# A delta rule in chunks: output as a stream of its own, and the inverse applied after the state's part

## The chip, the cores and the metric

The kernel runs on one core of a Trainium2 chip. The metric is the time of one execution on the device in microseconds (us). Engines are named as in the profile: PE is the tensor engine's matmul, PEld its weight load, DVE the vector engine, ACT the scalar engine, POOL is GpSimd, SP the queue that only issues DMAs. Each engine works through its own queue in order and waits there for what others have to deliver.

## What is computed

One inference step of a hybrid layer: 16 meta rows and 2048 prompt frames, and beside them 64 frames of a running stream. The input is projected; one half of the heads is latent attention, the other a gated delta rule with 4 heads of 128 x 128 state; then an output projection and an MLP. The delta rule is evaluated in chunks (here of 128 rows; 16 for the meta rows, 64 for the running stream, 18 chunks in all). Cut to what matters:

```python
decay = exp(where(causal, gc[:, None] - gc[None, :], -inf))     # gc: cumulative sum of g
a = where(strict, (k * beta) @ k.T * decay, 0)
t_inv = inverse(eye + a)
u = t_inv @ (v * beta)
w = t_inv @ (k * beta * exp(gc))
qk = q @ k.T * decay
# from chunk to chunk, with the state S:
v_new = u - w @ S
o = (q * exp(gc)) @ S + qk @ v_new
S = S * exp(gc[-1]) + (k * exp(gc[-1] - gc)).T @ v_new
# o is then normalised per row and multiplied by a gate
```

## The kernel before

The program has stages that follow each other: input projection and convolution (`phase_a`), the delta rule (`phase_g`), attention, attention of the running stream, output projection and MLP. The change is in `phase_g`, which runs from 519 to 950 us of the profile.

`phase_g` is written as generators that a loop advances in rounds; a `yield` ends a stream's part of a round. Three kinds of stream run side by side. `gdn_prep` prepares a chunk without needing the state: it loads k, v and q (L446, L448), transposes k and v (L455, L474), makes the decay matrix `dm` (L461, L463) and its scaled form `db`, normalises k (`rk`, `kn`, L485), forms the matrix to be inverted (`bn`, L500) and `qk` (L502), inverts by doubling over seven levels (`lev`, first mask L521, then L529 to L557), and ends with `uf`, the inverse (L574), and `wt`, the inverse's transpose applied to `kneg` = -k exp(gc) (L523, L578, L580). Up to four chunks are in preparation at once. `gdn_scan` takes one prepared chunk at a time, in six parts: `pv` = `uf` by `vn` (L598) plus `wt` by the state (L599) in one accumulation, `vw` (L601); the new state (L605, L607); the output's share of the state (L619, L621); its share of the chunk (L627, L629) with the row norm; the scaling on POOL (L638); the transpose (L642), the gate (L644) and the store. The third stream, `q_gen` (L728 to L742), projects and rotates the queries of attention in 17 tiles of five parts, and after it `keys` makes attention's first keys; one part of it is taken in each round after round `QS` = 5.

A new chunk is taken up at the earliest `GR` = 6 rounds after the one before, with at most `GK` = 4 in preparation and `GA` = 5 ahead of the scan. PSUM has five banks for the preparation (`gpp` in the trace), two for the scan (`gps`) and one for the queries. The order in which instructions stand in each engine's queue is then made by a scheduler, which follows the order of the code where it sees nothing better; operands are read by their names in the rows (`lev`, `bn`, `kn`, `vn`, `uf`, `vw`, `S`). Names and numbers of the constants are at L45 to L57.

Of the kernel before, what the change touches and what calls it, by code (L numbers as in the profile page):

```python
# [8 lines left out]
F32 = mybir.dt.float32  # L9
F32R = mybir.dt.float32r  # L10
# [36 lines left out]
GB = {"kq": 4, "qk": 5, "kd": 5, "vn": 5, "uf": 5, "wt": 5, "ss": 5, "kv": 2, "sq": 1, "kn": 1, "lg": 1, "dm": 2, "db": 1, "bn": 1,  # L47
      "kneg": 3, "bh": 4, "bl": 4, "tt": 5, "uu": 5, "q16": 2, "rk": 3, "se": 1, "vw": 2, "S": 3, "o1": 1, "o": 1, "fr": 2}
GR, GK, GA, GF, GL0 = 6, 4, 5, 2, 4
QSB, QS = 2, 5  # L50
# [60 lines left out]
def bc1(ap, p, a, b):  # L111
    return ap.unsqueeze(1).to_broadcast([p, a, b])
# [6 lines left out]
class Prog:  # L119
# [255 lines left out]
    def gdn_consts(self, es):  # L375
        nc, I = self.nc, self.I
        c = self.pool(es, "g_const")
        t = lambda name, shape, dt=F32: c.tile(list(shape), dt, name=name)
        self.m_le, self.m_gt = t("m_le", (128, 128)), t("m_gt", (128, 128))
# [6 lines left out]
        self.sct = {k: t(k, (128, nch, 4)) for k in ("beta", "nbeta", "g", "egc", "negc", "egl")}  # L386
        self.sc = {n: {k: v[:, i, :] for k, v in self.sct.items()} for i, n in enumerate(CHUNKS)}

    def gdn_setup(self):
# [32 lines left out]
        flat = lambda t: t.rearrange("p a b -> p (a b)")  # L422
        ps = self.aps.tile([128, NB], F32, name="ps", tag="ps", bufs=APB)
# [14 lines left out]
    def gdn_prep(self, n, P):  # L438
# [10 lines left out]
        lg = self.gt("lg", 2)  # L449
        nc.gpsimd.tensor_tensor(lg[:C, :, :C], bc1(self.m_gt[:C, :C], C, 4, C), bc2(sc["g"][:C], C, 4, C), op=ALU.mult)  # L450
# [9 lines left out]
        for h in range(4):  # L460
            nc.tensor.matmul(pe[:C, h, :C], lg[:C, h, :C], self.m_le[:C, :C], start=True, stop=True)  # L461
# [15 lines left out]
        if want_o:  # L477
            sq = self.gt("sq", 2)
            nc.scalar.activation(sq[:, :, :C], kq[:, :, 1, :C], AF.Square)
# [42 lines left out]
        kneg = self.gt("kneg", 1)  # L522
        nc.gpsimd.tensor_tensor(kneg[:C], kn[:C], bc2(sc["negc"][:C], C, 4, 128), op=ALU.mult)  # L523
# [57 lines left out]
        P.update(kq=kq, ss=ss, qk=qk, kd=kd, vn=vn, uf=uf, wt=wt)  # L581

    def gdn_scan(self, n, P):
# [17 lines left out]
        nc.vector.tensor_tensor(vw[:C], pv[:C], bc2(sc["beta"][:C], C, 4, 128), op=ALU.mult)  # L601
        yield
# [11 lines left out]
        if n == 0:  # L614
            return
        yield
        po = self.gpsum("s")
        for h in range(4):
            nc.tensor.matmul(po[:C, h, :], P["kq"][:, h, 1, :C], st[:, h, :], start=True, stop=True)  # L619
# [6 lines left out]
        for h in range(4):  # L626
            nc.tensor.matmul(po[:C, h, :], P["qk"][:C, h, :C], vw[:C, h, :], start=True, stop=True)  # L627
# [3 lines left out]
        for h in range(4):  # L631
            nc.scalar.activation(o1[:C, h, :], o[:C, h, :], AF.Square, accum_out=ss[:C, 4 + h:5 + h])
        fr = self.gt("fr", 1, (128, 12))
# [14 lines left out]
    def phase_g(self, g=True, q=True, eb=None):  # L648

        with ExitStack() as es:  # L650
# [12 lines left out]
            preps, scan, started, scanned, rounds = [], None, 0, 0, 0  # L663
            began = [-GL0] * NL
            while g and scanned < len(CHUNKS):
# [6 lines left out]
                if rounds > QS:  # L672
# [8 lines left out]
                if scan is None and "uf" in Ps[scanned]:  # L681
# [1249 lines left out]
```

## Time and profile before

| | before |
|---|---|
| median of 3 runs | 3322.38 us (3321.15 to 3323.21) |
| the profiled execution | 3322.66 us |
| its span | 3320.9 us |
| PE busy in the span | 96% |
| DVE, ACT, POOL busy | 80%, 47%, 12% |
| delta-rule stage, 519 to 950 us | 431 us |
| PE, DVE, POOL, ACT busy in the stage | 376.8, 310.5, 235.7, 214.5 us |

A row of the profile's timeline says when an instruction (or several of one kind) started, how long it took, the engine, the line of the kernel, what it writes and reads, and in brackets how long the engine sat idle before it and what ended that. A PE instruction's duration includes its way through the array, so what one costs the queue is the distance to the next start. PE needs two passes for one f32 product of this stage, so four heads appear as x8.

### The profile page before, as it was taken

How to read it: one execution, taken by the hardware profiler on the slowest of the kernel's cores; microseconds unless marked ns; L12 is line 12 of the kernel's file. 1: busy time of each engine (PE TensorE's matmuls, PEld its weight loads, DVE VectorE, ACT ScalarE, POOL GpSimd, SP SyncE). 2: the span in 40 equal slices, each digit the busy share in tenths (PEclk: the TensorE clock that was granted, in tenths of full speed). 3: DMA queues.
4: the chain of work that ended last, by engine and by line, in shares of the span. 5: the costliest groups of instructions: out<-in, count | busy, mean ns of one | idle time of the engine just before them, and what ended most of it. 6: DMA issues, size and time to landing. Idle time of an engine off the chain costs nothing.

```text
span 3320.9 us, 54512 instructions
## 1 busy us (share of the span) xinstructions
PE 3196.8 (96%) x20037; PEld 2943.1 (89%) x20037; DVE 2650.8 (80%) x5438; ACT 1558.4 (47%) x3495; POOL 400.5 (12%) x758
## 2 busy tenths in 40 slices
PE   9999998998979999999899999999999999999999
PEld 6888887888867778887799999999999999999999
DVE  8877654788758788888789888888888888988887
ACT  5555524555536868787564222334333333422232
POOL 0100013675510000000201000011000002100000
PEclk9999998999978999999999999999999999999999
DMA  4322213233221011010332222233222225122222
GB/s 132 91 74 70 74 63 100 87 104 100 59 57 35 20 34 34 25 37 26 106 99 75 77 77 75 76 110 109 88 76 73 65 73 160 58 73 77 77 74 70
DMA packets 318091, 248.09 MB, mean 75 GB/s; under 512 B 31776, under 2 KB 291616, under 8 KB 317760
## 3 DMA queue, kind: packets, MB, share of 16 engines
q1 hardware_dynamic: 300256, 219.21, 22.8%
q10 hardware_dynamic: 15536, 16.23, 1.6%
q0 software_dynamic: 2032, 9.18, 0.8%
q8 instruction: 157, 2.57, 0.3%
q14 instruction: 110, 0.90, 0.1%
HBM read 196.99 MB, written 47.52 MB: 74 GB/s over the span
## 4 chain that ended last, share of the span: by engine, by line
PE 83%; DVE 8%; ACT 2%; DMA 2%; issue 2%; POOL 1%; SPq 0%; POOLq 0%; DVEq 0%; ACTq 0%
PE psu L1601 23%; PE psd L1601 21%; PE ps L270 5%; PE ps L271 5%; PE ps L272 5%; PE pss L994 2%; PE pso L1011 2%; PE pss L995 2%; PE pss L996 2%; PE pso L1013 2%; PE pso L1012 2%; PE pspre L964 2%; DVE hl L1581 0%; PE psm L889 0%; DMA qh<-mrow 0%
## 5 line engine op out<-in xcount | busy, mean ns | idle before, releaser
L1601 PE MATMUL psu<-hh,uh 128*128 128x352 f32 x1728 | 563.0, 326 | 2.6 <-ACT uh L1497 2.1
L1601 PE MATMUL psu<-hl,uh 128*128 128x352 f32 x1728 | 557.3, 323 | 0.0
L1601 PE MATMUL psu<-hh,ul 128*128 128x352 f32 x1728 | 549.9, 323 | 0.0
L1601 PE MATMUL psd<-al,dh 128*128 128x352 f32 x1536 | 496.0, 323 | 3.5 <-DVE al L1790 3.2
L1601 PE MATMUL psd<-ah,dl 128*128 128x352 f32 x1536 | 494.6, 322 | 0.0
L1601 PE MATMUL psd<-ah,dh 128*128 128x352 f32 x1536 | 473.3, 324 | 11.1 <-DVE y L1709 7.4
L1709 DVE TENSOR_TENSOR y<-y,psd 128x352 f32<-128x352 f32 x768 | 386.6, 515 | 103.5 <-PE psd L1601 101.5
L1601 PEld LDWEIGHTS psu<-hh,uh 128*128 128x128 f32 x1728 | 325.7, 189 | 4.5 <-ACT uh L1497 2.5
L1601 PEld LDWEIGHTS psu<-hl,uh 128*128 128x128 f32 x1728 | 326.1, 189 | 1.2 <-issue 0.5
L1601 PEld LDWEIGHTS psu<-hh,ul 128*128 128x128 f32 x1728 | 323.9, 188 | 0.2 <-DVE ul L1475 0.2
L270 PE MATMUL ps<-hhi,whi 128*128 128x512 f32 (+5 forms) x880 | 313.6, 360 | 9.7 <-ACT hhi L134 7.1
L272 PE MATMUL ps<-hhi,wlo 128*128 128x512 f32 (+5 forms) x880 | 314.0, 358 | 0.0
L271 PE MATMUL ps<-hlo,whi 128*128 128x512 f32 (+5 forms) x880 | 312.5, 356 | 0.3 <-DVE hlo L135 0.2
L1601 PEld LDWEIGHTS psd<-ah,dh 128*128 128x128 f32 x1536 | 284.1, 188 | 16.9 <-DVE y L1709 11.5
L1601 PEld LDWEIGHTS psd<-al,dh 128*128 128x128 f32 x1536 | 289.1, 188 | 5.5 <-DVE al L1790 5.4
L1497 ACT CAST dh<-wr 128x512 fp32r<-128x512 f32 x192 | 119.3, 621 | 367.2 <-PE psd L1601 324.8
L1601 PEld LDWEIGHTS psd<-ah,dl 128*128 128x128 f32 x1536 | 288.8, 188 | 0.0
L1788 ACT CAST ah<-u 128x352 fp32r<-128x352 f32 x192 | 93.4, 487 | 398.6 <-DVE u L1786 280.0
L135 DVE TENSOR_TENSOR Pl<-P,Ph 128x512 fp32r<-128x512 f32 (+4 forms) x352 | 211.2, 611 | 52.2 <-ACT Ph L134 49.7
L998 ACT ACTIVATE P<-pss 128x512 f32<-128x512 f32 (+4 forms) x352 | 185.9, 539 | 87.6 <-PE pss L996 76.9
L965 DVE TENSOR_REDUCE mp<-pspre 128x1 f32<-128x296 f32 (+6 forms) x400 | 189.1, 500 | 31.1 <-PE pspre L964 29.2
L1714 POOL TENSOR_TENSOR y<-y,v 128x352 f32<-128x352 f32 x40 | 40.8, 1043 | 1330.8 <-DVE y L1709 1330.7
(458 smaller groups left out, 7266.5 us busy)
## 6 DMA issues: line engine op xcount, KB each, us to landing
wr<-in_w_up SPq DMA_DIRECT2D x192, 256.0 KB
wr<-in_w_down SPq DMA_DIRECT2D x192, 256.0 KB
qn<-scr_qN SPq DMA_DIRECT2D x32, 384.0 KB
wr<-in_w_out SPq DMA_DIRECT2D x48, 256.0 KB
wraw<-in_w_in SPq DMA_DIRECT2D x42, 256.0 KB
scr_convT<-s SPq DMA_DIRECT2D x36, 256.0 KB
mixr<-scr_mixT SPq DMA_DIRECT2D x12, 704.0 KB
out_y_T<-y SPq DMA_DIRECT2D x48, 176.0 KB
```

Of the source, the lines that this page charges most:

```text
L135: (lo_eng or nc.vector).tensor_tensor(lo, src, hi.bitcast(F32), op=ALU.subtract)
L270: nc.tensor.matmul(ps[:m, :n], whi[:, k, :m], hi[:, k], start=k == 0, stop=False)
L271: nc.tensor.matmul(ps[:m, :n], whi[:, k, :m], lo[:, k], start=False, stop=False)
L272: nc.tensor.matmul(ps[:m, :n], wlo[:, k, :m], hi[:, k], start=False, stop=k == 7)
L964: nc.tensor.matmul(ps[:, :z - a], qh[:r, i * 128:(i + 1) * 128], kh[:r, a:z], start=True, stop=True)
L965: nc.vector.tensor_reduce(m[:, i:i + 1] if one else mp[:, j:j + 1], ps[:, :z - a], axis=AX.X, op=ALU.max)
L994: nc.tensor.matmul(ps[:w, off:], kh[:r, s:s + w], qh[:r, off:], start=True, stop=False)
L998: nc.scalar.activation(p[:w, off:], ps[:w, off:], AF.Exp)
L1497: self.nc.scalar.copy(t[0], src)
L1601: self.nc.tensor.matmul(ps, w, h, start=i == 0, stop=i == len(steps) - 1)
L1709: adds.append(nc.vector.tensor_tensor(Y[j][:, d], Y[j][:, d], ps, op=ALU.add).ins)
L1788: done = nc.scalar.copy(A[f, j][0], u).ins
```

## The change

- `wt` and `kneg` are gone. The scan first multiplies the normalised keys by the state (`pk`), scales by -exp(gc) on DVE (`vk`), adds the values on POOL (`vr`), and applies the inverse once, to the sum (`pv`).
- The output is a generator of its own, `gdn_out`, in five parts; the scan has four, one of them empty. An output of a chunk is advanced in each round beside the scan of the next.
- The decay matrix: g is split into a rounded part `gh` and a rest `gl`; the mask `m_le` times each is made on POOL (two `lg` instead of one), and two fp32r matmuls of 512 columns take the place of four f32 ones of 128.
- In `gdn_prep` the norm's `rk`, its use in `kn`, and the square of q stand in other rounds than before.
- The third stream starts after round 2 instead of 5 and skips every sixth round. Six buffers of `kq` instead of four, two of `sq` and `lg` instead of one.

```diff
-GR, GK, GA, GF, GL0 = 6, 4, 5, 2, 4
-QSB, QS = 2, 5
+GR, GK, GA, GF, GL0, QE = 6, 4, 5, 2, 4, 6
+QSB, QS = 2, 2
...
+        nc.scalar.copy(self.sct["gh"], gg)
+        nc.vector.tensor_tensor(self.sct["gl"], gg, self.sct["gh"].bitcast(F32), op=ALU.subtract)
...
-        lg = self.gt("lg", 2)
-        nc.gpsimd.tensor_tensor(lg[:C, :, :C], bc1(self.m_gt[:C, :C], C, 4, C), bc2(sc["g"][:C], C, 4, C), op=ALU.mult)
+        lg = [self.gt("lg", 2, dt=F32R) for _ in range(2)]
+        for x, g in zip(lg, (sc["gh"].bitcast(F32), sc["gl"])):
+            nc.gpsimd.tensor_tensor(x[:C, :, :C], bc1(self.m_le[:C, :C], C, 4, C), bc2(g[:C], C, 4, C), op=ALU.mult)
...
-        for h in range(4):
-            nc.tensor.matmul(pe[:C, h, :C], lg[:C, h, :C], self.m_le[:C, :C], start=True, stop=True)
+        for i, x in enumerate(lg):
+            nc.tensor.matmul(pe[:C, :, :C], self.m_gt[:C, :C], x[:C, :, :C], start=i == 0, stop=i == 1)
...
+        if want_o:
+            sq = self.gt("sq", 2)
+            nc.scalar.activation(sq[:, :, :C], kq[:, :, 1, :C], AF.Square)
+        yield
         rk = self.gt("rk", 2, (128, 12))
...
-        yield
         tv = self.gpsum()
...
+        yield
         kn = self.gt("kn", 2)
...
-        kneg = self.gt("kneg", 1)
-        nc.gpsimd.tensor_tensor(kneg[:C], kn[:C], bc2(sc["negc"][:C], C, 4, 128), op=ALU.mult)
...
-        yield
-        ps = self.gpsum()
-        for h in range(4):
-            nc.tensor.matmul(ps[:, h, :C], kneg[:C, h, :], uf[:C, h, :C], start=True, stop=True)
-        wt = self.gt("wt", 2)
-        nc.scalar.copy(wt[:, :, :C], ps[:, :, :C])
...
+        pk = self.gpsum("s")
+        for h in range(4):
+            nc.tensor.matmul(pk[:C, h, :], P["kq"][:, h, 0, :C], st[:, h, :], start=True, stop=True)
+        vk = self.gt("vk", 1)
+        nc.vector.tensor_tensor(vk[:C], pk[:C], bc2(sc["negc"][:C], C, 4, 128), op=ALU.mult)
+        vr = self.gt("vr", 1)
+        nc.gpsimd.tensor_tensor(vr[:C], vk[:C], P["vn"][:C], op=ALU.add)
+        yield
+        yield
         pv = self.gpsum("s")
         for h in range(4):
-            nc.tensor.matmul(pv[:C, h, :], P["uf"][:C, h, :C], P["vn"][:C, h, :], start=True, stop=False)
-            nc.tensor.matmul(pv[:C, h, :], P["wt"][:, h, :C], st[:, h, :], start=False, stop=True)
+            nc.tensor.matmul(pv[:C, h, :], P["uf"][:C, h, :C], vr[:C, h, :], start=True, stop=True)
...
-        if n == 0:
-            return
-        yield
+
+    def gdn_out(self, n, P):
...
-                if rounds > QS:
+                if rounds > QS and rounds % QE:
...
+                if outs and next(outs[0], "x") == "x":
+                    outs.pop(0)
                 if scan is not None and next(scan, "x") == "x":
+                    if CHUNKS[scanned]:
+                        outs.append(self.gdn_out(CHUNKS[scanned], Ps[scanned]))
                     scan, scanned = None, scanned + 1
```

Where instructions stand now. On DVE, around the inverse's first mask of a late chunk (`lev<-m_lv,bn`; `gpp` and `gps` are PSUM banks), before:

```order
L634 TENSOR_SCALAR fr<-ss 128x4
L500 TENSOR_TENSOR bn<-gpp,db 128x256
L502 TENSOR_TENSOR qk<-gpp,dm 128x256
L644 SCALAR_TENSOR_TENSOR o_10181<-gps,g_out,ga 128x512
L521 COPY_PREDICATED lev_4990<-m_lv,bn 128x512
L601 TENSOR_TENSOR vw<-gps,beta 128x512
```

and on DVE there now:

```order
L507 TENSOR_TENSOR bn<-gpp,db 128x256
L509 TENSOR_TENSOR qk<-gpp,dm 128x256
L528 COPY_PREDICATED lev_4994<-m_lv,bn 128x512
L641 TENSOR_TENSOR o<-o_10143,gps 128x512
L600 TENSOR_TENSOR vk<-gps,negc 128x512
L562 CAST uu<-gpp 128x4x64
```

The output's gate product (L644) no longer stands ahead of the mask (L521, now L528), and `vk` is new behind it; the scan's `vw` has moved elsewhere.

On POOL, in the same part of the program, from the normalised keys' product `kd` on, before:

```order
L523 TENSOR_TENSOR kneg<-kn,negc 128x512
L525 TENSOR_TENSOR kd<-kn,dm 128x512
L638 TENSOR_TENSOR o<-o,fr 128x512
L507 TENSOR_TENSOR bl<-bn,bh 128x512
L595 TENSOR_TENSOR se<-S,egl 128x512
L450 TENSOR_TENSOR lg<-m_gt,g 128x512
```

and on POOL there now:

```order
L530 TENSOR_TENSOR kd<-kn,dm 128x512
L594 TENSOR_TENSOR se<-S,egl 128x512
L514 TENSOR_TENSOR bl<-bn,bh 128x512
L602 TENSOR_TENSOR vr<-vk,vn 128x512
L143 TENSOR_TENSOR fr<-fr 128x4
L455 TENSOR_TENSOR lg<-m_le,gh 128x512
L455 TENSOR_TENSOR lg<-m_le,gl 128x512
```

`kneg` is gone, `vr` stands behind `bl`, and there are two `lg`; the output's scaling (L638, now L651) stands ahead of `kd`.

On PE, at the end of the stage (the last chunk's scan and output, then attention's first matmuls, `pspre`), before:

```order
L598 MATMUL gps<-vn,uf 128x128
L599 MATMUL gps<-S,wt 128x128
L605 MATMUL gps<-vw,kd 128x128 x4
L619 MATMUL gps<-S,kq 128x128 x4
L627 MATMUL gps<-vw,qk 128x128 x4
L642 MATMUL gps<-ident,o 128x128 x4
L964 MATMUL pspre<-KTh_10679,qh 128x144
```

and on PE there now:

```order
L655 MATMUL gps<-ident,o 128x128 x4
L607 MATMUL gps<-vr,uf 128x128 x4
L614 MATMUL gps<-vw,kd 128x128 x4
L631 MATMUL gps<-S,kq 128x128 x4
L639 MATMUL gps<-vw,qk 128x128 x4
L655 MATMUL gps<-ident,o 128x128 x4
L940 MATMUL psm<-ident,kn 105x128
L981 MATMUL pspre<-KTh_11047,qh 128x144
```

One group of four (L607) stands where four pairs of L598 and L599 did, still behind the transpose of the chunk before (L655, before L642), and a transpose of attention's keys (L940) has come behind the last of them.

## Rows read from the trace of the kernel before

**Rows 1.** The page: busy us, share, instructions; a group's busy, mean ns, idle.

```profile
PE 3196.8 (96%) x20037; PEld 2943.1 (89%) x20037; DVE 2650.8 (80%) x5438; ACT 1558.4 (47%) x3495; POOL 400.5 (12%) x758
...
L135 DVE TENSOR_TENSOR Pl<-P,Ph 128x512 fp32r<-128x512 f32 (+4 forms) x352 | 211.2, 611 | 52.2 <-ACT Ph L134 49.7
```

**Rows 2.** L446: duration in ns (least, median, most), first and last start.

```profile
L446 SPq DMA_DIRECT2D kv<-scr_convT x18: 359/360/499, 519.6 to 858.4; - x18
```

**Rows 3.** Stretches: length, busy us of each engine, PE clock, DMA share, GB/s.

```profile
519.00:950.00 431.00, 376.82 (x3698) 337.96 (x3698) 310.48 (x656) 214.54 (x759) 235.71 (x450) 0.94 0.33 89
604.50:884.00 279.50, 255.91 (x2654) 233.16 (x2652) 224.66 (x478) 153.22 (x548) 173.48 (x335) 0.97 0.34 95
...
720.00:760.00 40.00, 33.80 (x372) 30.73 (x371) 34.62 (x71) 18.99 (x69) 24.70 (x54) 1.00 0.32 87
832.90:850.00 17.10, 15.55 (x184) 14.38 (x184) 13.19 (x29) 9.08 (x35) 9.92 (x17) 1.00 0.31 78
```

**Rows 4.** PE's timeline, 836 to 842: start, length, line, operands, idle before.

```profile
836.38 1.06 PE L461 MATMUL gpp<-m_le,lg 128*128 128x128 f32 x8
837.28 1.06 PE L627 MATMUL gps<-vw,qk 128*128 128x128 f32 x8
...
840.82 1.14 PE L578 MATMUL gpp<-uf,kneg 128*128 128x128 f32 x8
841.79 0.40 PE L541 MATMUL gpp<-tt,bh 128*128 128x64 f16 x8
```

**Rows 5.** PE's timeline, 846.5 to 849.5.

```profile
846.51 0.39 PE L598 MATMUL gps<-vn,uf 128*128 128x128 f32 x2
...
848.30 0.28 PE L546 MATMUL gpp<-lev,uu 128*128 128x64 f16 x4
...
849.41 0.40 PE L529 MATMUL gpp<-id,lev 128*128 128x128 f16 x4 [0.48 <-DVE lev L521]
```

**Rows 6.** DVE's timeline, L601 alone: the first scan, four late ones, the last.

```profile
604.54 0.67 DVE L601 TENSOR_TENSOR vw<-gps,beta 16x512 f32<-16x512 f32 x1
...
832.16 0.68 DVE L601 TENSOR_TENSOR vw<-gps,beta 128x512 f32<-128x512 f32 x1
...
849.27 0.68 DVE L601 TENSOR_TENSOR vw<-gps,beta 128x512 f32<-128x512 f32 x1
...
883.99 0.68 DVE L601 TENSOR_TENSOR vw<-gps,beta 128x512 f32<-128x512 f32 x1
...
900.88 0.68 DVE L601 TENSOR_TENSOR vw<-gps,beta 128x512 f32<-128x512 f32 x1
...
939.84 0.69 DVE L601 TENSOR_TENSOR vw<-gps,beta 128x512 f32<-128x512 f32 x1 [1.90 <-PE gps L599]
```

**Rows 7.** The mask L521 over the stage; POOL and DVE around one of them.

```profile
L521 DVE CAST_PREDICATED lev<-m_lv,bn x18: 215/682/1648, 559.2 to 899.4; 128x512 f16<-128x512 uint8 x16, 16x64 f16<-16x64 uint8 x1, 64x256 f16<-64x256 uint8 x1
...
842.70 1.04 POOL L523 TENSOR_TENSOR kneg<-kn,negc 128x512 f32<-128x512 f32 x1
...
847.65 1.16 POOL L507 TENSOR_TENSOR bl<-bn,bh 128x512 f16<-128x512 f32 x1 [1.90 <-ACT bh L506]
...
847.83 1.53 DVE L521 CAST_PREDICATED lev<-m_lv,bn 128x512 f16<-128x512 uint8 x1
```

**Rows 8.** PE's timeline, the last two outputs.

```profile
929.01 1.06 PE L578 MATMUL gpp<-uf,kneg 128*128 128x128 f32 x8
929.91 1.06 PE L627 MATMUL gps<-vw,qk 128*128 128x128 f32 x8
936.03 1.12 PE L642 MATMUL gps<-ident,o 128*128 128x128 f32 x4 [5.07 <-POOL o L638]
...
948.87 1.12 PE L642 MATMUL gps<-ident,o 128*128 128x128 f32 x4 [5.12 <-POOL o L638]
```

**Rows 9.** PE's timeline, two of attention's fp32r matmuls.

```profile
962.80 0.39 PE L995 MATMUL pss<-ql,KTh 96*128 96x512 f32 x1
963.03 0.39 PE L996 MATMUL pss<-qh,KTl 96*128 96x512 f32 x1
```

More of the change, by code (lines that the diff above doesn't have):

```diff
@@ L46 @@
 GL, QLS = 17, 20
-GB = {"kq": 4, "qk": 5, "kd": 5, "vn": 5, "uf": 5, "wt": 5, "ss": 5, "kv": 2, "sq": 1, "kn": 1, "lg": 1, "dm": 2, "db": 1, "bn": 1,
-      "kneg": 3, "bh": 4, "bl": 4, "tt": 5, "uu": 5, "q16": 2, "rk": 3, "se": 1, "vw": 2, "S": 3, "o1": 1, "o": 1, "fr": 2}
-GR, GK, GA, GF, GL0 = 6, 4, 5, 2, 4
-QSB, QS = 2, 5
+GB = {"kq": 6, "qk": 5, "kd": 5, "vn": 5, "uf": 5, "ss": 5, "kv": 2, "sq": 2, "kn": 1, "lg": 2, "dm": 2, "db": 1, "bn": 1,
+      "vk": 1, "vr": 1, "bh": 4, "bl": 4, "tt": 5, "uu": 5, "q16": 2, "rk": 3, "se": 1, "vw": 2, "S": 3, "o1": 1, "o": 1, "fr": 2}
+GR, GK, GA, GF, GL0, QE = 6, 4, 5, 2, 4, 6
+QSB, QS = 2, 2
 EARLY = {"lath0": 1, "latl0": 1, "kr0": 1, "ssr0": 1, "V0": 2, "KTh0": 2, "KTl0": 2, "raw": 1, "rt": 1,
@@ L378, in gdn_consts @@
         t = lambda name, shape, dt=F32: c.tile(list(shape), dt, name=name)
-        self.m_le, self.m_gt = t("m_le", (128, 128)), t("m_gt", (128, 128))
+        self.m_le, self.m_gt = t("m_le", (128, 128)), t("m_gt", (128, 128), F32R)
         self.m_lv = t("m_lv", (128, 8, 128), U8)
@@ L385, in gdn_consts @@
         self.nc.gpsimd.memset(self.bt, 0.0)
-        self.sct = {k: t(k, (128, nch, 4)) for k in ("beta", "nbeta", "g", "egc", "negc", "egl")}
+        self.sct = {k: t(k, (128, nch, 4)) for k in ("beta", "nbeta", "g", "egc", "negc", "egl", "gl")}
+        self.sct["gh"] = t("gh", (128, nch, 4), F32R)
         self.sc = {n: {k: v[:, i, :] for k, v in self.sct.items()} for i, n in enumerate(CHUNKS)}
@@ L477, in gdn_prep @@
         if want_o:
-            sq = self.gt("sq", 2)
-            nc.scalar.activation(sq[:, :, :C], kq[:, :, 1, :C], AF.Square)
             pn = self.gpsum()
@@ L574, in gdn_prep @@
         nc.vector.tensor_tensor(uf[:C, :, :C], u[:C, :, :C], ps[:C, :, :C], op=ALU.add)
-        yield
-        ps = self.gpsum()
-        for h in range(4):
-            nc.tensor.matmul(ps[:, h, :C], kneg[:C, h, :], uf[:C, h, :C], start=True, stop=True)
-        wt = self.gt("wt", 2)
-        nc.scalar.copy(wt[:, :, :C], ps[:, :, :C])
-        P.update(kq=kq, ss=ss, qk=qk, kd=kd, vn=vn, uf=uf, wt=wt)
+        P.update(kq=kq, ss=ss, qk=qk, kd=kd, vn=vn, uf=uf)
     def gdn_scan(self, n, P):
@@ L595, in gdn_scan @@
         nc.gpsimd.tensor_tensor(se, st, bc2(sc["egl"], 128, 4, 128), op=ALU.mult)
+        pk = self.gpsum("s")
[7 more added lines that the diff above has]
+        yield
         pv = self.gpsum("s")
         for h in range(4):
-            nc.tensor.matmul(pv[:C, h, :], P["uf"][:C, h, :C], P["vn"][:C, h, :], start=True, stop=False)
-            nc.tensor.matmul(pv[:C, h, :], P["wt"][:, h, :C], st[:, h, :], start=False, stop=True)
+            nc.tensor.matmul(pv[:C, h, :], P["uf"][:C, h, :C], vr[:C, h, :], start=True, stop=True)
         vw = self.gt("vw", 2)
         nc.vector.tensor_tensor(vw[:C], pv[:C], bc2(sc["beta"][:C], C, 4, 128), op=ALU.mult)
+        P.update(st=st, vw=vw)
         yield
@@ L613, in gdn_scan @@
             nc.scalar.dma_start(O["s_S"].rearrange("h k v -> k h v"), new)
-        if n == 0:
-            return
-        yield
+    def gdn_out(self, n, P):
+        nc, S = self.nc, self.S
+        t0, C = chunk_span(n)
+        sc = self.sc[n]
         po = self.gpsum("s")
         for h in range(4):
-            nc.tensor.matmul(po[:C, h, :], P["kq"][:, h, 1, :C], st[:, h, :], start=True, stop=True)
+            nc.tensor.matmul(po[:C, h, :], P["kq"][:, h, 1, :C], P["st"][:, h, :], start=True, stop=True)
         o1 = self.gt("o1", 1)
@@ L626, in gdn_scan @@
         for h in range(4):
-            nc.tensor.matmul(po[:C, h, :], P["qk"][:C, h, :C], vw[:C, h, :], start=True, stop=True)
+            nc.tensor.matmul(po[:C, h, :], P["qk"][:C, h, :C], P["vw"][:C, h, :], start=True, stop=True)
         o = self.gt("o", 1)
@@ L632, in gdn_scan @@
             nc.scalar.activation(o1[:C, h, :], o[:C, h, :], AF.Square, accum_out=ss[:C, 4 + h:5 + h])
+        yield
         fr = self.gt("fr", 1, (128, 12))
@@ L662, in phase_g @@
             Ps = [{"first": i < NL} for i in range(len(CHUNKS))]
-            preps, scan, started, scanned, rounds = [], None, 0, 0, 0
+            preps, outs, scan, started, scanned, rounds = [], [], None, 0, 0, 0
             began = [-GL0] * NL
-            while g and scanned < len(CHUNKS):
+            while g and (scanned < len(CHUNKS) or outs):
                 if rounds >= max((started - GF) * GR, began[started % NL] + GL0) and len(preps) < GK and started < min(len(CHUNKS), scanned + GA):
@@ L680, in phase_g @@
                         ek = self.early_keys = self.keys(0, 0)
-                if scan is None and "uf" in Ps[scanned]:
+                if scan is None and scanned < len(CHUNKS) and "uf" in Ps[scanned]:
                     scan = self.gdn_scan(CHUNKS[scanned], Ps[scanned])
+                if outs and next(outs[0], "x") == "x":
+                    outs.pop(0)
                 if scan is not None and next(scan, "x") == "x":
+                    if CHUNKS[scanned]:
+                        outs.append(self.gdn_out(CHUNKS[scanned], Ps[scanned]))
                     scan, scanned = None, scanned + 1
```

## The prediction

> **What bounds the kernel now.** I read the page first: TensorE (PE) is busy for 96% of 3320.9 us [rows 1]. The change touches one stage only, the delta-rule stage, so the share that counts is that stage's. The first load of L446 is issued at 519.6 us and the last output transpose, L642, stands at 948.87 [rows 2, 8]. The reader should see in the table of stretches [rows 3] that nothing saturates there: from 519 to 950, PE is busy for 376.8 of 431 us, the vector engine (DVE) for 310.5, POOL for 235.7, ACT for 214.5. From 604.5 to 884.0, between the first scan (L601, the row on `vw`) and the fourteenth, the shares are 92%, 80%, 62% and 55%. A busy PE row is padded there by modelled ends, so 92% is an upper figure: in the period that ends with the second row of [rows 5] PE stops for 0.48 us, and what it waits for is DVE's L521. So the stage is set by in-order queues that hand work to each other, PE first and DVE close behind. The highest share of DVE that I found in a 40-us stretch is 34.62 of 40, 87% [rows 3]; it is reached while the query tiles (L728 to L742) run beside the chunks.
>
> Two regimes and a tail follow from the scan's own row. The thirteen intervals between scans from 604.54 to 883.99 take 21.5 us each in the mean; late in that stretch, with no query tile beside it, one takes 17.1 us (832.16 to 849.27). The last three, from 900.88 to 939.84, take 13.0 us each [rows 6]. There PE waits 5.07 and 5.12 us for the output's normalisation on POOL (L638) before it may transpose [rows 8], and PE's queue holds the next chunk's L598 behind that transpose.
>
> **The change part by part.** PE, per full chunk. L578 (the product of `kneg` and `uf`) goes: it holds PE from 840.82 to 841.79, 0.97 us. L598 and L599 together hold it from 846.51 to 848.30, 1.79 us for 16 passes; what replaces them is two groups of 8 such passes, `pk` and `pv`, 0.90 each. L461 holds PE from 836.38 to 837.28, 0.90; two fp32r matmuls of 512 columns replace it. None such stands in this stage; attention's, 128x512 with fp32r operands, follow each other by 0.23 us (962.80 to 963.03), so 0.46. Sum: 3.66 us out, 2.26 in, **1.40 us less PE per chunk** [rows 4, 5, 9].
>
> DVE gains one instruction per chunk, `vk`, a product from PSUM like L601: 0.68 us [rows 6]. ACT loses the copy of `wt`; with ACT at half of the stage I count that as nothing. POOL loses `kneg` (L523, 1.04 us) and gains `vr` and a second `lg`, both of that shape: 1.04 more per chunk at 62% busy [rows 3, 7]. `vr` is on the scan's path, but between `pk` and `pv` the changed order has the inverse's products of two chunks, so the way of 0.90 + 0.68 + 1.04 us has cover; with the cover gone it would cost those 2.6 us a chunk, and only the last chunks come near that.
>
> The rounds. The old DVE order puts the output's last product (L644) between the last `qk` (L502) and the inverse's first mask (L521), for which PE waits. In the changed order the mask follows `qk` directly or after one short row in most chunks; `vk` stands ahead of it in 2 of 18. By that one place a period could gain the 0.48 us and more, and a cost may appear at the same place, since PE has less of its own left to cover the mask: one `pk`, 0.90, where L598 and L599 gave 1.79. DVE bounds what can come of it: it carries 13.19 us of work in a period of 17.10 [rows 3], with `vk` 13.87, and at its highest share, 87%, that allows no period under 15.9.
>
> A rule of the skill speaks against the added POOL work. The row first: L521 takes 0.68 us in the median, but the one at 847.83 takes 1.53, until 849.36; POOL's L507 had begun 0.18 us before it and ended at 848.81 [rows 7]. The Trainium skill, SBUF — State Buffer, "Who interferes with whom", says that a VectorE instruction with two SBUF inputs and a GpSimd instruction that reads SBUF take the same read port, and the later one is blocked until the other is done; by that, the trace agrees. What it would do here is a rival below, priced from these rows.
>
> The sum, against the profiled execution's own 3322.66 us (span 3320.9; the runs' median, 3322.38, is 0.3 lower).
> - The thirteen intervals to 884.0. By PE: 13 x 1.40 = 18.2 us less, if it stays as busy. By DVE: its 224.7 us of work grow by 13 x 0.68 to 233.5, and at 87% this needs 268.5 us instead of 279.5, so 11 less. I take **-12**, nearer to DVE's, because the wait that the period shows at the mask ends on DVE.
> - The last chunks. L578 (929.01 to 929.91) stands in the chain ahead of L627, and L598 with L599 behind the transpose fall to one group: 1.8 us less in each of three intervals, and about half a microsecond in the one before: **-6**. The chain from L627 to L642 stays.
> - The start, 519 to 604.5: one or two chunks' PE work, -2, against query weights that are prepared some rounds earlier: 0.
> - Attention's first keys. In the changed order two transposes of the second head's keys stand behind the last output transpose. Bounds: nothing, if the loads that open attention hide them, and two splits of L135, 0.61 us each by its mean [rows 1]; I take **+1**.
> Total -17: 3322.66 - 17 = 3305.7, less the 0.3 to the median: **3305 us**.
>
> The query tiles' skipped rounds I count at nothing. The code spreads the tiles to round 107, but in the order that the scheduler made the last one stands before the ninth scan instead of the seventh. Work is moved by two chunks, not removed; it may fill PE's waits there, which is in the range.
>
> **The rivals.**
> - *PE alone sets the pace, and the rounds take the waits too.* For: PE's 92%. Then 18.2 us plus 13 x 0.48 for the wait on L521 come off, 24, with the tail's 6 and +1: 3322.4 - 29 = 3293. Against: DVE would need 91% and more (233.5 of 255), above anything that I found in the trace.
> - *The slots become waits.* PE's freed time is spent waiting for the same DVE and POOL results, as `vk` and `vr` lengthen the way from the state to `pv`; the periods stay and only the tail pays: -6 + 1, 3317 us. For: the 0.48 us end on DVE, and the cover there shrinks. Against: L578 and half of L598/L599 lie ahead of results that DVE waits for.
> - *Slower: the port.* DVE sets the pace at the share that it has now, 80%, and the extra POOL instruction blocks one two-input DVE instruction per chunk for 1.53 - 0.68 = 0.85 us. Then 13 x 0.68 / 0.80 = 11 and 17 x 0.85 = 14 come on, with -6 and +1: +20, 3342 us. It decides once DVE does not rise above its present 80%. Against: the instruction that blocks L521 in the row, L507, is there already and stays.
> - The change doing less than it says: the scheduler, not the rounds, sets the final order. That is the spread of the tiles above, and it is inside the main case.
>
> **How the numbers follow.** Main case (3296 to 3312) 0.48; PE alone 0.20; slots become waits 0.20; the port 0.12. A difference under 0.2% (6.6 us) is about what a measurement of this kernel can't tell from none. Faster by more: 0.48 + 0.20 = 0.68. Same: 0.20. Slower: 0.12. The range reaches down past the first rival's centre to 3287, and up over the second's to the start of the slower side, 3327; it leaves out most of the port's case and a corner of the first rival, not quite 0.2.
>
> **What would show it.** Right: the stage from the first load to the last transpose takes 411 to 417 us instead of 429, periods without query tiles 15.9 to 16.5, DVE's share in the middle rises from 80% to between 84 and 87%, the last three intervals fall to about 11. PE alone: a share of DVE over 88%. Slots become waits: periods of 17 us with new waits of PE on `vr` or on the mask. Port: more masks and rotations at twice their shortest time, DVE at 80% or less. All of it would be wrong if attention, whose own code does not change, came out more than 4 us different: its order is made by the same scheduler, and I assume that this does not matter.

## The result, and the profile after

The changed kernel takes **3341.9 us** in the median (3338.2 to 3347.5, 4 runs), the kernel before 3322.5: a ratio of 1.0060, 95% interval 1.0043 to 1.0078. It is 19 us slower where 17 us faster was forecast, and outside the range. The profiled execution of the changed kernel is its longest, 3347.5 us (span 3345.5); so a difference between the two profiles holds some 5 us more than one between medians.

From the page of the changed kernel, the row of engines:

```profile
PE 3196.0 (96%) x19785; PEld 2933.6 (88%) x19785; DVE 2653.9 (79%) x5457; ACT 1551.0 (46%) x3478; POOL 427.0 (13%) x776
```

Stretches of the changed kernel, in columns as in [rows 3]: the stage to its last transpose, first to fourteenth scan, the end of the stage, attention, the rest:

```profile
519.00:959.50 440.50, 366.75 (x3433) 324.31 (x3432) 311.72 (x672) 204.10 (x739) 260.26 (x465) 0.89 0.31 87
593.20:886.70 293.50, 253.01 (x2469) 226.01 (x2467) 222.22 (x488) 146.75 (x538) 194.97 (x355) 0.93 0.32 91
903.00:959.50 56.50, 40.08 (x383) 37.22 (x381) 30.45 (x63) 14.11 (x59) 16.55 (x29) 0.80 0.19 51
...
959.50:1615.20 655.70, 624.34 (x3210) 502.98 (x3210) 523.29 (x1281) 491.42 (x1096) 18.45 (x45) 0.95 0.12 31
1615.20:3345.50 1730.30, 1697.16 (x10540) 1675.04 (x10540) 1451.03 (x2836) 595.95 (x1171) 96.55 (x121) 0.99 0.28 85
```

The same three parts of the kernel before:

```profile
519.00:948.90 429.90, 375.72 (x3693) 336.86 (x3692) 310.48 (x656) 214.54 (x759) 235.47 (x449) 0.94 0.33 89
...
948.90:1597.50 648.60, 622.00 (x3208) 505.42 (x3208) 521.93 (x1279) 488.88 (x1094) 18.00 (x44) 0.95 0.12 32
1597.50:3320.90 1723.40, 1691.23 (x10540) 1669.56 (x10540) 1450.76 (x2836) 595.61 (x1171) 97.22 (x121) 1.00 0.28 85
```

The span grew by 24.6 us: 10.6 in the stage, 7.1 in attention, 6.9 behind it. So more than half of it lies behind the stage, in code that the change doesn't touch. A second profile with the same order of instructions on every engine (e15 below, 3341.1 us, nearer to the median) gives 4.8 in the stage, 6.7 in attention and 6.6 behind it. In the stage PE's row is busy 9 us less, at a lower granted clock: 0.89 after 0.94. Late scans of the changed kernel, DVE's timeline, as in [rows 6]:

```profile
886.70 0.68 DVE L609 TENSOR_TENSOR vw<-gps,beta 128x512 f32<-128x512 f32 x1
...
903.02 0.68 DVE L609 TENSOR_TENSOR vw<-gps,beta 128x512 f32<-128x512 f32 x1
...
948.19 0.69 DVE L609 TENSOR_TENSOR vw<-gps,beta 128x512 f32<-128x512 f32 x1 [0.96 <-PE gps L607]
```

The first scan is 11.3 us earlier than in [rows 6]. The thirteen intervals behind it take 293.5 us instead of 279.5, the last three 45.2 instead of 39.0.

**PE's time in three parts.** A busy row doesn't say whether PE works, works at half speed or waits. For each PE instruction I took the distance to the next one's start. Its *work* is the lower quartile of that distance for its line and shape at full clock; what a stretch at 1.2 GHz adds, up to as much again, is *lengthening*; the rest is *waiting*. The granted clock has two levels, 1.2 and 2.4 GHz. What the lower one does shows in PE's timeline of the changed kernel:

```profile
782.93 1.25 PE L639 MATMUL gps<-vw,qk 128*128 128x128 f32 x8 [2.95 <-DVE S L616]
...
797.78 0.70 PE L841 MATMUL psm<-ident,rt 32*80 32x32 f32 x5 [3.09 <-DMA rt<-out_p_ropeT]
...
801.68 2.06 PE L505 MATMUL gpp<-kq 128*128 128x256 f32 x4
803.53 1.00 PE L655 MATMUL gps<-ident,o 128*128 128x128 f32 x4
...
805.70 1.02 PE L505 MATMUL gpp<-kq 128*128 128x256 f32 x4
806.56 0.28 PE L546 MATMUL gpp<-tt,bh 128*128 128x64 f16 x4
```

```profile
783.90:787.30 3.40, 2.99 (x21) 2.18 (x19) 2.83 (x8) 1.79 (x10) 1.69 (x3) 0.50 0.30 120
794.10:804.30 10.20, 7.10 (x53) 6.35 (x53) 6.69 (x20) 4.29 (x10) 4.56 (x12) 0.50 0.41 130
```

L505 holds PE for 1.85 us at 801.68, inside the stretch of clock 0.50 (second fence), and for 0.86 at 805.70, behind it. A wait of 2.95 us stands ahead of the first such stretch. The table gives the stage, from 519 to the last transpose, from one profile of each kernel (the experiments e1 to e18 follow):

| kernel | median, us | stage | work | lengthening | waiting | time at 1.2 GHz |
|---|---|---|---|---|---|---|
| before | 3322.5 | 429.9 | 321.4 | 16.1 | 92.5 | 51 |
| changed | 3341.9 | 440.5 | 294.7 | 30.2 | 115.5 | 94 |
| e1 old pace | 3332.9 | 437.5 | 294.6 | 28.8 | 114.2 | 87 |
| e2 one stream | 3359.0 | 464.4 | 298.9 | 39.5 | 126.1 | 116 |
| e3 algebra only | 3349.1 | 455.4 | 303.8 | 29.1 | 122.3 | 85 |
| e4 stream only | 3343.2 | 454.7 | 322.8 | 36.7 | 95.2 | 96 |
| e5 algebra, six parts | 3360.3 | 460.3 | 303.2 | 32.8 | 124.5 | 99 |
| e6 own store buffer | 3318.3 | 422.3 | 296.7 | 25.6 | 100.3 | 81 |
| e7 f32 decay | 3338.3 | 422.2 | 302.4 | 19.4 | 100.5 | 61 |
| e8 thin dummies | 3348.7 | 448.8 | 325.9 | 42.7 | 80.0 | 111 |
| e9 dense dummies | 3327.1 | 425.4 | 311.8 | 17.9 | 95.8 | 61 |
| e10 five `kq` | 3317.9 | 422.3 | 295.5 | 21.9 | 104.7 | 70 |
| e11 own store, f32 | 3310.5 | 410.8 | 304.5 | 17.2 | 89.3 | 53 |
| e12 own store, old pace | 3326.9 | 422.0 | 296.9 | 24.1 | 101.1 | 77 |
| e13 changed, loads swapped | 3325.3 | 430.6 | 296.4 | 29.9 | 104.3 | 90 |
| e14 before, loads swapped | 3349.2 | 439.0 | 319.6 | 26.0 | 93.3 | 72 |
| e15 changed, `kd` early (same queues as changed) | 3340.1 | 434.7 | 295.7 | 25.1 | 114.1 | 77 |
| e16 before, `kd` early | 3322.5 | 428.6 | 320.6 | 17.6 | 90.4 | 54 |
| e17 same order, 4 dummies | 3340.3 | 432.8 | 309.8 | 19.4 | 103.6 | 60 |
| e18 same order, 8 dummies | 3361.9 | 450.8 | 326.0 | 21.9 | 103.0 | 63 |

The first two rows hold the result: **PE's work fell by 26.7 us, waiting rose by 23.0 and lengthening by 14.1.** The work that the change removes was gone, and the stage was longer all the same. How far a single profile carries shows in e15, whose queues are those of the changed kernel: its stage is 5.8 us shorter, its lengthening 5.1 us less and its time at 1.2 GHz 17 us less, while work and waiting agree within 1.4 us. Smaller differences between two rows than these show nothing. Of PE's idle gaps, those that a result of DVE ended grew from 30.9 to 40.5 us.

### The profile page after: what moved, and what is told of

Same layout as the page of the kernel before. It is cut to its first block, busy times and chain, and to the rows that moved or that the text cites. A ratio compares the mean times of both kernels' runs of the same rounds, so it can differ in the third digit from the quotient of the medians.

```text
span 3345.5 us, 54014 instructions
## 1 busy us (share of the span) xinstructions
PE 3196.0 (96%) x19785; PEld 2933.6 (88%) x19785; DVE 2653.9 (79%) x5457; ACT 1551.0 (46%) x3478; POOL 427.0 (13%) x776
## 4 chain that ended last, share of the span: by engine, by line
PE 82%; DVE 9%; DMA 3%; ACT 2%; issue 2%; POOL 2%; SPq 0%; ACTq 0%; POOLq 0%; DVEq 0%
PE psu L1618 23%; PE psd L1618 21%; PE ps L270 5%; PE ps L271 5%; PE ps L272 5%; PE pss L1011 2%; PE pso L1028 2%; PE pso L1030 2%; PE pss L1012 2%; PE pss L1013 2%; PE pso L1029 2%; PE pspre L981 2%; DMA scr_mixT<-o 1%; DMA qh<-mrow 1%; DVE hl L1598 1%
```

## Experiments: the parts of the change alone

The first theory was a new wait. The output product `o1` (L633) and the stored product (L657) share one buffer, so in the changed kernel DVE waits for a store. From DVE's and from PE's waits in the stage (total, times, longest):

```profile
DVE o L633 <- DMA scr_mixT<-o: 11.3, 8, 2.8
```

```profile
PE gpp L534 <- DVE lev L528: 13.1, 8, 3.5
PE gps L655 <- POOL o L651: 11.6, 5, 5.1
...
PE gps L598 <- DVE o L633: 5.0, 4, 2.6
```

PE's waits in the kernel before:

```profile
PE gps L642 <- POOL o L638: 10.8, 3, 5.1
...
PE gpp L529 <- DVE lev L521: 8.7, 11, 1.8
```

**e1, the old pace.**

```diff
-GR, GK, GA, GF, GL0, QE = 6, 4, 5, 2, 4, 6
-QSB, QS = 2, 2
+GR, GK, GA, GF, GL0, QE = 6, 4, 5, 2, 4, 99999
+QSB, QS = 2, 5
```

> The changed kernel with the query tiles paced as before: the third stream starts after round 5 and no round is skipped. The rest of the change stays. Theory A (the new output stream: DVE's first output product waits for the store of the output before it, and the queues behind it wait too) expects no change in that wait and a total within 5 us of the changed kernel's 3342. Theory B (the pacing: query tiles now run to 784 us instead of 753, and they and attention's first keys fall between dependent steps) expects the stage from first load to last transpose to come back from 441 to 430 us or less, total 3325 to 3332. Theory C (the inverse applied behind the state's part makes the chain from state to state longer) expects no change: 3338 to 3346.

3332.9 us, ratio 1.0024 (1.0013 to 1.0035). The stage gives back 3 us, not the 10 of theory B, and two profiles of the changed kernel's own order differ by more. In the profiles 3.9 us come back in attention and 7.8 behind it, where PE is at 1.2 GHz for 17 us instead of 32.

**e2, the output at the end of the scan's stream.**

```diff
-                    if CHUNKS[scanned]:
-                        outs.append(self.gdn_out(CHUNKS[scanned], Ps[scanned]))
...
+        yield
         po = self.gpsum("s")
```

> The changed kernel with the output put back at the end of the scan's stream, so that an output is made before the next scan begins; algebra, decay matrix and pacing stay as changed. The scan's stream now has nine parts a chunk. Theory A (output stream) expects that the waits of DVE for the store go (11 us in the changed kernel) and the stage takes 430 us or less, total 3325 to 3332. Theory B (pacing) and theory C (algebra) expect no gain, and a loss of some us, since nine parts are more than the six rounds between two chunks: 3342 to 3355.

3359.0 us, 1.0101 (1.0087 to 1.0116). DVE no longer waits for the store, and yet the stage is 24 us longer, against theory A.

**e3, the algebra alone, in the kernel before.** Its buffers are not quite those of before: `kq` has six instead of four, as in the changed kernel.

```diff
-            nc.tensor.matmul(pv[:C, h, :], P["uf"][:C, h, :C], P["vn"][:C, h, :], start=True, stop=False)
-            nc.tensor.matmul(pv[:C, h, :], P["wt"][:, h, :C], st[:, h, :], start=False, stop=True)
+            nc.tensor.matmul(pk[:C, h, :], P["kq"][:, h, 0, :C], st[:, h, :], start=True, stop=True)
...
+        yield
+            nc.tensor.matmul(pv[:C, h, :], P["uf"][:C, h, :C], vr[:C, h, :], start=True, stop=True)
```

> The kernel before with the algebra alone: state product, its scaling on DVE, the sum with the values on POOL, then one product with the inverse, in the scan's own stream (one part more than before, seven); no output stream, old pacing, old decay matrix. Theory C (algebra) expects this to be as slow as the changed kernel, 3335 to 3345. Theories A and B expect PE's 0.97 us a chunk less work to show, stage 420 to 429 us, total 3312 to 3322.

3349.1 us, 1.0075 (1.0062 to 1.0088). PE's work fell by 17.6 us (17 chunks by 0.97 is 16.5) and the stage grew by 25.5. Late intervals, from the eleventh scan to the fourteenth, take 19.6 to 20.5 us instead of 17.1 to 17.6. PE's timeline in one such period:

```profile
859.39 0.63 PE L489 MATMUL gpp<-ident,kn 128*128 128x128 f32 x4 [1.36 <-DVE fr L634]
...
866.85 0.40 PE L527 MATMUL gpp<-id,lev 128*128 128x128 f16 x4 [1.28 <-DVE lev L521]
868.37 0.28 PE L544 MATMUL gpp<-lev,uu 128*128 128x64 f16 x4 [1.12 <-DVE lev L540]
```

Three waits of over a microsecond stand where the period before had 0.48 and less [rows 5].

**e4, the output's stream alone, in the kernel before.**

```diff
-        yield
-        po = self.gpsum("s")
+    def gdn_out(self, n, P):
+        po = self.gpsum("s")
...
+                        outs.append(self.gdn_out(CHUNKS[scanned], Ps[scanned]))
```

> The kernel before with the output as a stream of its own beside the next scan, and nothing else changed. Theory A (output stream, one buffer for the first output product and the stored one) expects the wait of DVE for the store to appear, some 10 us in the stage, and the total at 3330 to 3340. Theories B and C expect the total within 6 us of the kernel before, 3316 to 3328.

3343.2 us, 1.0059 (1.0040 to 1.0079). DVE waits 5.4 us for the store, half of what theory A expected, and the total lies above the range of either. PE's work and waiting are those of before within 3 us; the stage is 25 us longer, 20.6 of it lengthening. The profile is its longest run (3351.7), so part of this is the run's.

**e5, the algebra without the seventh part.** Against e3:

```diff
         nc.gpsimd.tensor_tensor(vr[:C], vk[:C], P["vn"][:C], op=ALU.add)
-        yield
         pv = self.gpsum("s")
```

> The kernel before with the algebra alone, as in the third experiment, but the state product, the sum with the values and the product with the inverse are written in one part, so that the scan keeps six parts a chunk instead of seven. In the third experiment PE's work in the stage fell by 17.6 us while the stage grew by 25.5; a late period without query tiles took 19.8 to 20.0 us where before took 17.1, and 20.0 / 17.1 is 7 / 6. Theory R (a chunk's period is the number of its scan's parts times the length of a round, some 2.85 us, and not PE's work) expects periods near 17.1 and a total within 5 us of the kernel before, 3319 to 3328. Theory C (the longer chain from state to state: state product, DVE, POOL, then the inverse, 2.6 us more) expects periods of 19 to 20 us and 3340 to 3350, as with seven parts.

3360.3 us, 1.0118 (1.0101 to 1.0136). Theory R falls: six parts, and the same late intervals of 20.6 to 21.7 us. This fits the longer way from state to state, whatever the number of parts, but it doesn't show it alone: e3 and e5 both have the six `kq`, and e10 below shows that one `kq` more or less can move a kernel by 24 us. The algebra with four `kq` was not run.

## Experiments: small edits, and a control

**e6, a buffer for the store.**

`GB` gets an entry `"mx": 1`; five `kq` instead of six make room.

```diff
-        mx = self.gt("o1", 1)
+        mx = self.gt("mx", 1)
```

> The changed kernel with a buffer of its own for the gated output that is stored, so that the next output's first product no longer waits for a store to land; one buffer of the keys and queries less (five) makes room. Theory A (that wait, 11.3 us of DVE in the stage of the changed kernel) expects the stage at 430 us or less instead of 440.5 and the total at 3328 to 3334. Theory R (rounds and order set the period) and the theory that the tensor engine's low clock after pauses is what costs expect the stage within 4 us of the changed kernel's, 3336 to 3346.

3318.3 us, 0.9985 (0.9974 to 0.9997): 24 us less than the changed kernel, on the side of theory A and more than its 3328 to 3334.

**e10, the control: `"kq": 5` in `GB` instead of 6, and no buffer for the store.**

> Control for the store's own buffer: the changed kernel with five buffers of keys and queries instead of six, and nothing else. If the gain of 24 us in the sixth experiment came from the store's buffer, this stays at 3336 to 3346 with the stage at 438 to 444 us and DVE's wait for the store at about 11 us. If it came from the other order that any change of a buffer makes, this too falls to 3315 to 3330.

3317.9 us, 0.9993 (0.9983 to 1.0003), the same stage of 422.3 us, and the wait is still there:

```profile
DVE o L633 <- DMA scr_mixT<-o: 8.3, 7, 1.7
```

So theory A falls: the wait is real, but taking it away was not needed for the 24 us. One `kq` buffer less gives them, by itself or by the order that follows from it: from 519 to 1650 us a quarter of PE's instructions stand elsewhere in its queue.

**e7, the old decay matrix.** One `lg`, made as before, and:

```diff
-        for i, x in enumerate(lg):
-            nc.tensor.matmul(pe[:C, :, :C], self.m_gt[:C, :C], x[:C, :, :C], start=i == 0, stop=i == 1)
+        for h in range(4):
+            nc.tensor.matmul(pe[:C, h, :C], lg[:C, h, :C], self.m_le[:C, :C], start=True, stop=True)
```

> The changed kernel with the decay matrix as before: one product on POOL and four f32 matmuls instead of two products and two fp32r matmuls of 512 columns. PE gets some 0.5 us a chunk more, POOL 1.04 less. If the added POOL work is what costs (my rival of the port), the total falls by 10 to 14 us, to 3328 to 3332, and fewer DVE instructions take twice their shortest time. If PE's work counts, it rises by 5 to 8 us, to 3347 to 3350. If neither counts, it stays at 3336 to 3346.

3338.3 us, 1.0034 (1.0014 to 1.0054), 4 us less than the changed kernel and no difference that can be told. Its profile is one of its shortest runs (3326.7), so the 422 us of stage flatter it.

**e11, both** (e7's edit and the `mx` of e6, with six `kq`).

> The changed kernel with both: the store's own buffer and the f32 decay matrix of before (six buffers of keys and queries). Each of the two alone brought the stage to 422 us in its profile, and in both DVE's wait for the store is gone (0 and 0.7 us). If the wait was the common cause, together they bring no more: stage 418 to 426 us, total 3315 to 3325. If the f32 decay acted by POOL and the port, a gain of its own, both together come to 404 to 412 us and 3300 to 3310.

**3310.5 us, 0.9966 (0.9954 to 0.9979): the one version that beats both kernels.** Its stage, 410.8 us, is what the prediction gave the changed kernel (411 to 417). The result is also close to what was expected if the old decay matrix gains by POOL and the shared port; but DVE instructions that take over 1.8 times the shortest of their kind are 51 in its stage, 52 in e6, 54 in e10 and 41 in the changed kernel, so a relief of the port doesn't show. The order changed here too, and what gained is open.

**e12, the store's buffer and the old pace** (the edits of e6 and e1).

> The changed kernel with the store's own buffer and the query tiles paced as before. The pacing undone alone gave 3 us of the stage and 9 of the total. If the two are separate, the total comes to 3309 to 3316, below both kernels. If the pacing's 9 us were the order of attention and the clock of that run, it stays at 3316 to 3322.

3326.9 us, 1.0006 (0.9995 to 1.0018). The stage is that of e6 (422.0); the total is 9 us longer, where e1 was 9 us shorter. The pace has no effect of its own that these runs can tell.

**e13 to e16, the same instructions written in another order.** Two edits that change no instruction, each in both kernels: `kq`'s load written ahead of `kv`'s (the diff), and `kd` written ahead of the products with the keys.

```diff
-        nc.sync.dma_start(kv[:, :, :C], cv[:, 4:12, t0:t0 + C])
         nc.sync.dma_start(kq[:, :, 1, :C], cv[:, 0:4, t0:t0 + C])
+        nc.sync.dma_start(kv[:, :, :C], cv[:, 4:12, t0:t0 + C])
```

> The changed kernel with the two loads of a chunk written in the other order (keys and queries first, then keys and values); the same instructions, and some 400 lines of another order in the engines' queues. If the 19 us are the change's own, the stage stays at 436 to 445 us and the total at 3336 to 3348. If they are an unlucky order, the stage comes to 420 to 430 us and the total to 3316 to 3330.

> The same swap of the two loads in the kernel before. If the order alone moves either kernel by 15 us and more, and the kernel before stands at a good one, its stage grows from 430 to 440 us and more, total 3330 to 3345. If order matters little, it stays within 5 us, 3317 to 3327.

> The changed kernel with the product kd written ahead of the two products with the keys instead of behind the inverse's first mask; the same instructions in another order. The change's own loss: stage 436 to 445 us, total 3336 to 3348. An unlucky order: stage 415 to 432 us, total 3312 to 3330.

> The same move of kd in the kernel before. Good order lost: stage 438 us and more, total 3328 to 3345. Order matters little: within 5 us, 3317 to 3327.

With the loads swapped, the changed kernel takes 3325.3 us (1.0006, 0.9993 to 1.0020) and **the kernel before 3349.2 (1.0074, 1.0047 to 1.0100)**: with that order the change would have been 24 us faster. With `kd` early they take 3340.1 (1.0048, 1.0032 to 1.0064) and 3322.5 (0.9997, 0.9986 to 1.0009). These two are hardly other orders: by the traces e15 has the changed kernel's order on every engine, since the scheduler undid the edit, and e16 differs from before only in that `kneg` and `kd` change places on POOL. They are repeats, and they agree with the first runs within 2 us. In e13 a fifth and in e14 a third of PE's instructions stand elsewhere. An order alone moves the kernel before by 27 us (e14) and the changed one by 17 (e13), and a buffer less moves that by 24 (e10). The orders that really differ are few: 3322 and 3349 us for before; 3342, 3333 (e1), 3318 (e10) and 3325 (e13) for the changed kernel. Whether the change as such gains or loses is not settled by so few; that 19 us lie inside what an order does is shown.

## Experiments: more work for PE

These add matmuls whose results are overwritten.

**e8, thin dummies.** The q norm's product (L488, one column wide) three times:

```diff
+            for _ in range(3):
                 for h in range(4):
                     nc.tensor.matmul(pn[:C, 0, h:h + 1], sq[:, h, :C], self.ones[:, 0:1], start=True, stop=True)
```

> The changed kernel with dummy work on PE: the q norm's product is made three times instead of once, which is some 1.8 us more for PE in each of 17 chunks, off the path from state to state, and brings PE's work in the stage back to what it was before the change (about 321 us at full clock; the changed kernel has 295). If PE's work sets the pace, the stage grows by 25 to 31 us, total 3367 to 3373. If waits between engines set it, the stage grows by less than 10 us. If the low clock that follows PE's pauses is a cost of its own (in the stage 30 us of lengthened matmuls against 16 before), the added work fills pauses, the low-clock time falls below the 94 us of the changed kernel, and the total stays or falls: 3330 to 3344.

3348.7 us, 1.0079 (1.0060 to 1.0099). 31 us more work on PE, 7 us more time: waiting fell by 35, and the time at 1.2 GHz rose from 94 to 111 us, against the theory of the clock. It looks as if PE's work didn't set the pace, but the order moved with the dummies; e17 keeps it.

**e9, dense dummies, scheduled anew.**

```diff
+        for _ in range(4):
+            nc.tensor.matmul(pe[:C, :, :C], self.m_gt[:C, :C], lg[0][:C, :, :C], start=True, stop=True)
```

> The changed kernel with other dummy work on PE: ahead of the two fp32r matmuls of the decay matrix, four more of the same kind (512 columns, 0.23 us each) write the same bank and are overwritten; 0.9 us a chunk, some 16 us in the stage, dense columns where the earlier filler had single ones. By the runs so far a kernel's time multiplied by its granted clock is 3253 us for before, 3248 for the changed kernel and 3245 with the earlier filler, so the clock (0.979, 0.972, 0.969) carries the difference. If PE's thin work is what brings the low clock, the low-clock time in the stage falls well below 94 us and the total to 3325 to 3338. If the low clock only follows waits whose length the other engines set, it stays at 80 to 110 us and the total at 3338 to 3352.

3327.1 us, 1.0018 (1.0009 to 1.0027): **more work, 15 us less time**. The order moved here too, so two runs put the same dummies into PE's finished queue:

**e17 and e18, dense dummies, every other instruction where it was.**

```diff
+    for i in blk.instructions:
+        if i.opcode == "Matmult" and i.start_tensor_calc and i.ins[0].memref.startswith("lg_"):
+            for k in range(4):
+                seq.append(copy(f"I-{9000000 + len(seq)}", True, type(sync)(on_wait=list(sync.on_wait), on_update=[]) if k == 0 else None))
```

> The changed kernel with every instruction in the same place of its queue, and four dense dummy matmuls (fp32r, 512 columns, 0.23 us each at full clock) put ahead of the first decay-matrix matmul of each chunk, 0.9 us a chunk, 16 in the stage. If PE's work sets the pace, the stage grows from 440 to 456 us, total 3352 to 3360. If PE's low clock after thin work costs time of its own, the low-clock time in the stage falls from 94 to 60 us or less and the total falls to 3325 to 3336, as with the same dummies in a newly scheduled order (3327). If only the order counts, the dummies vanish in PE's waits or lengthen the chain a little: stage 438 to 446 us, 3338 to 3348.

> The same with eight dummies, 1.8 us a chunk, 31 in the stage, which is as much as PE's work fell by the change. PE sets the pace: stage 470 us, total 3368 and more. The clock is a cost of its own: low-clock time lower still than with four, total 3325 to 3342. Only the order counts: 3340 to 3356, with the low-clock time where it was.

The stage in e17 and in e18:

```profile
519.00:951.80 432.80, 368.95 (x3506) 326.28 (x3504) 310.92 (x672) 206.23 (x739) 261.15 (x465) 0.93 0.32 89
```

```profile
519.00:969.80 450.80, 386.81 (x3579) 341.58 (x3577) 313.52 (x672) 206.69 (x739) 260.39 (x465) 0.93 0.31 85
```

By the traces PE's queue holds 72 instructions more in e17 and every engine's order is otherwise that of the changed kernel. e17 takes 3340.3 us, 1.0053 (1.0040 to 1.0065), as the changed kernel does within 2 us: **15 us of added work cost nothing.** Against the two profiles with the same queues (changed and e15) waiting fell by 11.9 and 10.5 us, lengthening by 10.8 and 5.7, and the time at 1.2 GHz from 94 and 77 to 60. So most of the added work went into PE's waits. The time at 1.2 GHz fell as the theory of the clock expected; the total did not come to its 3325 to 3336 but to what the third theory, only the order counts, gave (3338 to 3348). That the clock is a cost of its own is therefore not shown by the total, and the 13 us by which e9 is shorter are the order's. The next four dummies (e18, 3361.9 us, 1.0117, 1.0101 to 1.0132) cost 22: waiting and lengthening fall no further. The likely reason, not shown, is that the dummies stand ahead of the decay matrix that others wait for.

## Why the prediction was wrong, point by point

- **The bound: PE first, at 92%, and DVE close behind.** The first wrong step. The prediction called the share padded and still costed by it. Of the 429.9 us of the stage PE's work takes 321.4 at full clock, 75%. That waits are handed on between queues was a sentence of the prediction but no term of its sum. In e17, with every queue kept, 15 us of work more on PE cost nothing, so PE's work alone doesn't set the length of the stage.
- **Thirteen intervals, -12: measured +14.** The term rested on work removed (1.40 us a chunk, nearly right: 26.7 us over the stage, 24 by the prediction) and on DVE rising to 87%. DVE's share fell to 222.2 of 293.5, 76%. Waits took the room (23.0 us more in the stage) and slower matmuls (14.1). PE's largest wait is at the mask, 13.1 us instead of 8.7, though the prediction argued that it would stand freer; most of the 23.0 us is spread over many places.
- **`vr` covered, else 2.6 us a chunk.** The price fits e3 and e5, where nothing covers it: late intervals of 19.6 to 21.7 us instead of 17.1 to 17.6, though those two have six `kq` as well. In the changed kernel the same three take 16.0, 21.6 and 22.6, so the cover that the prediction counted on doesn't show. That the output's stream covers part is suggested by e2, 17 us slower without it, in another order. `vr` itself takes 1.28 us in the median, not 1.04.
- **The last chunks, -6: measured +6.2** in the three intervals and +2.3 behind them. The half microsecond in the interval before came off (0.6). The clock is 0.80 there, from 903.0 to 959.5, and was 0.94 over the last 56.5 us of the stage before. The longer way from state to `pv` is uncovered there, as the prediction had warned; how much of the 6.2 is its own isn't separated.
- **The start, 0: measured -11.3**; the thirteen intervals behind it are 14.0 longer.
- **Attention, +1: measured +7.1.** The last line of the prediction assumed that the scheduler's order of attention doesn't matter. One place holds more than all of it: two heads' ends (the last sum `osum`) stand 61.3 us apart instead of 50.1. e14, the kernel before with two loads swapped, has the same 61.3 in the same place, so it comes with the order and not with the algebra:

```profile
1276.00:1337.00 61.00, 58.30 (x314) 47.73 (x312) 45.93 (x120) 47.30 (x116) 2.78 (x9) 0.94 0.12 32
```

The changed kernel:

```profile
1276.00:1337.00 61.00, 58.13 (x313) 47.46 (x311) 46.26 (x121) 46.93 (x115) 2.78 (x9) 0.94 0.12 32
```

- **Behind attention, no term: measured +6.9.** PE is at 1.2 GHz for 32 us of that part instead of 17. Over all twenty profiles its length goes with that time: 1723 to 1725 us where it is 13 to 17 us, 1730 to 1731 us where it is 32 to 35. All four profiles with the changed kernel's order (changed, e15, e17, e18) have 32 us there; which part of the order does it is open.
- **The rival of the port gave 3342 us: the right number by luck.** Its condition held (DVE not above 80%), but its sign did not come: masks of over 1.4 us are 4 of 18 now and were 7, and of all DVE instructions in the stage 41 take over 1.8 times the shortest of their kind, where 59 did before. One POOL product less (e7) gains 4 us, no difference that can be told. A single pair as in [rows 7] (1.53 us for the mask instead of 0.68) fits the rule of the Trainium skill, SBUF — State Buffer, "Who interferes with whom"; a cost of it in the total doesn't show.
- **The rival that the slots become waits** was nearest in mechanism: PE's freed time did turn into waits, on DVE above all. It had no term for the lengthening (14.1 us) nor for the code behind the stage, and so ended at no change.
- **What no term had: the order.** The prediction costed the edits one by one and looked up the new queues at a few places only. The schedule is made anew, and of the two orders of the kernel before that were run it stands at the better (3322 against 3349).

Still open: which pairs in the order make the 15 to 24 us. Five `kq`, dense dummies and swapped loads all find a better one, and no rule here tells it ahead. So the step that failed is known, and the cause of the waits that took its place is not.

## What to carry to other kernels

Where a scheduler orders the queues, first make two or three edits that change no instruction and time them: an effect inside their spread (here up to 27 us) can't be put down to what an edit does. Compare the queues, too: of four such edits here one left every queue as it was and one only swapped two neighbours on POOL. Split the busy row of an engine into work, lengthening by the clock and waiting before you call it the bound. If dummies put into its finished queue cost nothing, that much work is not what the time is made of, and taking as much away need not gain. Where a step is moved onto the way from state to state, count it there, and let another stream cover it.

## What was not expected of the hardware

Time follows the granted clock from run to run of one program. In 89 runs of the kernel before, on four chips, it goes from 3316.4 us at 0.982 to 3332.8 at 0.974; a line through them falls by 2.0 to 2.4 us for each 0.001 of clock on every chip. The changed kernel's four runs stand at 0.974 in the median, before at 0.979; by that line this is an estimate of some 10 of the 19 us. The line says that the two go together, not which makes the other: a run with longer waits could lose both. What the traces of the stage show is that the changed kernel, with 26 us less work on PE, spends 77 to 94 us at 1.2 GHz instead of 51, and that its matmuls are lengthened by 25 to 30 us instead of 16.
